# One flag of the tile scheduler: the order of every engine's instructions built with its timeline account of time

## The chip, the cores and the metric

The kernel runs on one core of one Trainium2 chip. The metric is the device time of one execution in microseconds (us). The core has five engines that matter here: TensorE (PE in the profile, with its weight loads as PEld), VectorE (DVE), ScalarE (ACT), GpSimd (POOL) and SyncE (SP), which here only issues DMAs. Each engine works through a list of instructions of its own, and waits on semaphores where it needs another engine's result.

## What is computed

A decoder block of depth 1 over a sequence of 1024 tokens of width 1024, in f32:

```
z = rms_norm(h, ln_mix_g) @ w_in
y_sgu  = sgu_group(z[..., :1536], ...)
y_rwkv = rwkv7_group(z[..., 1536:], ...)
h = h + concat([y_sgu, y_rwkv]) @ w_out
h = h + mem_cross_attention(h, mem, ...)
return rms_norm(h, ln_f_g)
```

The part that sets the order of work is `rwkv7_group`: 8 heads of 64, each with a 64x64 state that is carried from token to token:

```
sa = einsum('bhvk,bhk->bhv', state, a)
state = state * w + sa[..., None] * bb + v[..., None] * k
y = einsum('bhvk,bhk->bhv', state, r)
```

## The kernel before, in words

**Dense products.** Every large matrix product is split in three: both operands are divided into a high and a low part (`split`, L156 on ACT and L157 on DVE), and `mm3` (L177 to L179) issues three matmuls of 128x512 or 128x256 into a PSUM tile `mm`, of which there are three. There are 3216 such matmuls in the program. They are called dense products here. The stages are: keys and values of the memory, input norm and the first projections; the SGU group; the RWKV group with the rest of the input projection and the first part of the output projection (`out_proj`); then the rest of `out_proj` with the folding of the key weights (`k_fold`), the folding of the value weights, and the attention over eight blocks of tokens.

**The RWKV group.** The work is cut into four pairs of heads and two halves of the sequence, eight pieces that follow each other; a piece is called a half here. A half has eight chunks of 64 tokens. `serial` carries the state through the chunks, 64 chunks in all, each in three steps that depend on each other:

```
nc.tensor.matmul(us[:, 0, :], ra[:, c, :, :], s_old, ...)      # L766, then DVE L768 makes ab
nc.tensor.matmul(us[:, 1, :], tt[...], ab, ...)                # L775, then ACT L776 makes avt
nc.tensor.matmul(us[:, 2, :], bkt[:, cq, :], avt[:, cq, :], ...) # L781, then DVE L787 makes s_new
```

From L766 to L775, from L775 to L781, and from L781 to the next chunk's L766 are called hops. They are 183 in all. What a half needs before its chunks is made one or two halves ahead: `elementwise` (L583 to L636), `grams` (L656 to L684), `turn` (L696, L702) and `solve` (four rounds of small products at L717 with DVE between them). In `grams` the masked blocks go to DRAM and come back in another layout (L665, L672); then 28 small DVE instructions that depend on each other (L677, L679) invert 16x16 blocks after L673, and the result goes to DRAM and back again (L680, L684) before `solve` begins with L725. After a half, `outputs` (L799) and `finish` (L809 to L828) write its rows to `y_scr` in DRAM.

**What sets the order.** The function `drive` calls the generators of these pieces in turn, so that dense products, steps of the chain and the small work are recorded mixed with each other. That is the program order; instruction numbers and the numbers in tile names grow with it. When the `TileContext` of `kernel()` (L1198) is left, a scheduler makes one list per engine out of it: among what its account of time says is ready, what was recorded earlier goes first. It also adds the waits. The lists are fixed when the kernel is built, and an engine does not leave its list's order when an instruction has to wait.

## Time and profile before

| what | value |
|---|---|
| median of 3 runs | 954.45 us (954.15 to 956.72) |
| the profiled execution, its own time | 952.35 us |
| its span in the profile | 950.6 us |
| PE busy | 906.8 us |
| DVE busy | 593.5 us |
| ACT busy | 390.5 us |

The span is from the first to the last instruction; the execution's own time holds 1.75 us more. Busy time is the time in which an engine has at least one instruction under way. Matmuls overlap in the array, so a row's duration of one matmul (0.39 us for a dense product) is longer than the time from its start to the next one's.

### The profile page before, as it was taken

What the parts mean: (1) busy time and instruction counts of PE and PEld (TensorE: products, weight loads), DVE (VectorE), ACT (ScalarE), POOL (GpSimd) and SP (SyncE); (2) the same over time, 40 slices, a digit from 0 to 9 for tenths busy, and PEclk for the clock granted to TensorE, in tenths of its full rate; (3) what the DMA queues carried; (4) which work ended last, traced back from release to release, by engine and by line L of the source; (5) the groups of instructions that cost most, each with busy time, mean ns of one, the idle gap of its engine ahead of it and who ended that gap; (6) DMA issues with size and microseconds to landing.
All of it is one profiled execution on the core that took longest, in us unless ns stands there. A gap on an engine that the chain in (4) does not pass through costs nothing.

```text
span 950.6 us, 16113 instructions
## 1 busy us (share of the span) xinstructions
PE 906.8 (95%) x6236; PEld 728.1 (77%) x6236; DVE 593.5 (62%) x1375; ACT 390.5 (41%) x818; POOL 50.5 (5%) x115
## 2 busy tenths in 40 slices
PE   6989999999999999898989999999799999999996
PEld 6978888888777777676767677677698778888885
DVE  5867233334585878686868789867587664444333
ACT  6763222224442525252616272534266553333222
POOL 0001000012000000000000000000000000000000
PEclk9999999999999999999999999999999999999999
DMA  8862011113122112121111084425462400000001
GB/s 314 264 216 89 23 67 67 67 68 111 40 55 44 37 26 60 26 59 26 48 35 49 24 240 113 115 52 151 143 212 70 136 6 2 26 26 26 26 32 45
DMA packets 86092, 76.86 MB, mean 81 GB/s; under 512 B 38272, under 2 KB 58752, under 8 KB 86016
## 3 DMA queue, kind: packets, MB, share of 16 engines
q1 hardware_dynamic: 84864, 73.73, 24.9%
q10 hardware_dynamic: 1152, 2.10, 0.6%
q8 instruction: 49, 0.80, 0.4%
q14 instruction: 27, 0.22, 0.1%
HBM read 62.17 MB, written 13.64 MB: 80 GB/s over the span
## 4 chain that ended last, share of the span: by engine, by line
PE 78%; DVE 13%; issue 3%; DMA 2%; POOL 2%; ACT 1%; POOLq 0%; SPq 0%; DVEq 0%; ACTq 0%
PE mm L177 21%; PE mm L179 20%; PE mm L178 20%; PE cb L717 3%; PE us L766 2%; PE us L775 2%; PE yps L799 2%; PE us L781 1%; POOL grs L153 1%; DVE gr L666 1%; PE co L717 1%; DVE stdiag L787 1%; DMA w_raw<-in_w_sv 1%; DVE cs L592 1%; PE co L432 1%
## 5 line engine op out<-in xcount | busy, mean ns | idle before, releaser
L177 PE MATMUL mm<-xh,w_hi 128*128 128x512 f32 x400 | 167.2, 418 | 0.0
L179 PE MATMUL mm<-xh,w_lo 128*128 128x512 f32 x400 | 159.8, 400 | 0.0
L178 PE MATMUL mm<-xl,w_hi 128*128 128x512 f32 x400 | 159.5, 399 | 0.0
L157 DVE TENSOR_TENSOR w_lo<-w_raw,w_hi 128x512 fp32r<-128x512 f32 x115 | 78.7, 686 | 63.9 <-ACT w_hi L156 61.4
L156 ACT CAST w_hi<-w_raw 128x512 fp32r<-128x512 f32 x115 | 70.8, 617 | 91.4 <-PE mm L178 75.8
L179 PEld LDWEIGHTS mm<-xh,w_lo 128*128 128x128 f32 x400 | 75.8, 190 | 14.8 <-issue 0.2
L177 PEld LDWEIGHTS mm<-xh,w_hi 128*128 128x128 f32 x400 | 76.0, 190 | 12.9 <-issue 1.0
L178 PEld LDWEIGHTS mm<-xl,w_hi 128*128 128x128 f32 x400 | 76.2, 190 | 12.5 <-issue 0.5
L177 PE MATMUL mm<-wo,w_hi 128*128 128x512 f32 x128 | 54.2, 424 | 0.0
L776 ACT COPY avt<-us 64x128 f32<-64x128 f32 x64 | 16.6, 259 | 90.1 <-PE us L775 89.8
L178 PE MATMUL mm<-wo,w_hi 128*128 128x512 f32 x128 | 52.4, 409 | 0.0
L179 PE MATMUL mm<-wo,w_lo 128*128 128x512 f32 x128 | 51.8, 404 | 0.0
L177 PE MATMUL mm<-vp_h,p_hi 128*128 128x512 f32 x128 | 51.3, 401 | 0.0
L179 PE MATMUL mm<-kp_h,w_lo 128*128 128x512 f32 x128 | 50.1, 391 | 0.0
L177 PE MATMUL mm<-kp_h,w_hi 128*128 128x512 f32 x128 | 50.0, 391 | 0.0
L179 PE MATMUL mm<-vp_h,p_lo 128*128 128x512 f32 x128 | 50.0, 390 | 0.0
L178 PE MATMUL mm<-vp_l,p_hi 128*128 128x512 f32 x128 | 49.9, 390 | 0.0
L178 PE MATMUL mm<-kp_l,w_hi 128*128 128x512 f32 x128 | 49.9, 389 | 0.0
L787 DVE SCALAR_TENSOR_TENSOR stdiag<-us,dc,sd 64x64 f32<-64x64 f32 x112 | 31.6, 283 | 21.9 <-PE us L781 19.4
L772 ACT ACTIVATE sd<-stdiag,dc 128x128 f32<-128x128 f32 x56 | 22.4, 399 | 40.7 <-DVE stdiag L787 37.1
L1040 DVE TENSOR_REDUCE mx<-mm 128x2 f32<-128x512 f32 x16 | 11.1, 691 | 41.8 <-PE mm L179 41.8
L499 ACT ACTIVATE t<-mm,vec 128x512 f32<-128x512 f32 x34 | 23.3, 684 | 33.7 <-PE mm L179 32.7
(272 smaller groups left out, 2029.1 us busy)
## 6 DMA issues: line engine op xcount, KB each, us to landing
w_raw<-in_w_blk SPq DMA_DIRECT2D x50, 256.0 KB, 2.5
w_raw<-y_scr SPq DMA_DIRECT2D x32, 256.0 KB, 3.3
w_raw<-in_w_kv SPq DMA_DIRECT2D x17, 256.0 KB, 3.9
xr<-in_xT SPq DMA_DIRECT2D x8, 512.0 KB, 5.7
w_raw<-in_w_out SPq DMA_DIRECT2D x16, 256.0 KB, 2.8
h_all<-in_x SPq DMA_DIRECT2D x16, 256.0 KB, 4.5
pr<-in_w_qT SPq DMA_DIRECT2D x8, 512.0 KB, 4.4
w_raw<-in_w_o SPq DMA_DIRECT2D x16, 256.0 KB, 2.6
```

The lines of the kernel that those rows point to most:

```text
L156: nc.scalar.copy(out=hi, in_=src)
L157: (eng or nc.vector).tensor_tensor(out=lo, in0=src, in1=hi.bitcast(F32), op=ALU.subtract)
L177: nc.tensor.matmul(ps, lh, rh, start=first, stop=False)
L178: nc.tensor.matmul(ps, lh, rl, start=False, stop=False)
L179: nc.tensor.matmul(ps, ll, rh, start=False, stop=last)
L499: nc.scalar.activation(out=t1[:, 1:HT + 1], in_=ps, func=AF.Copy, scale=vc("mu", b))
L717: nc.tensor.matmul(ps[R[hh], c, :], fl(hh, c), fr(hh, c), start=True, stop=True)
L766: nc.tensor.matmul(us[:, 0, :], ra[:, c, :, :], s_old, start=True, stop=True)
L772: nc.scalar.activation(out=sd, in_=s_old, func=AF.Copy, scale=dcc)
L775: nc.tensor.matmul(us[:, 1, :], tt[:, c - c % 2:c - c % 2 + 2, :], ab, start=True, stop=True)
L787: nc.vector.scalar_tensor_tensor(out=s_new[h2, h2], in0=us[h2, 2, h2], scalar=dcc[h2], in1=sd[h2, h2], op0=ALU.mult, op1=ALU.add)
L799: nc.tensor.matmul(yps[R[c % 2], o:o + 64], gr[:, c, hh, :], avt[:, c, R[hh]], start=True, stop=True)
```

## The change

`TileContext` takes a flag that says with which account of time the scheduler builds its order. Nothing else is changed: the same instructions are recorded, in the same program order, with the same tiles and buffers. On every engine the two lists hold the same instructions.

```
-    with tile.TileContext(nc) as tc:
+    with tile.TileContext(nc, schedule_with_timeline_sim=True) as tc:
         tile_hybrid_block(tc, *args)
```

All five lists change: a PE instruction stands 58 places from where it stood on average (of 4893), a DVE instruction 21 (of 1377), an ACT instruction 10 (of 770), one of SP 5 (of 330). Three places follow.

The first is PE in the sixth half, from the second step of its second chunk to the third chunk (`us_5659` and `us_5767` are the PSUM tiles of these chunks; `mm_` are dense products, L823 and L799 belong to `finish` and `outputs`). Before:

```order
L775 MATMUL us_5659<-abdiag1_1927,tt_5441 128x128
L179 MATMUL mm_5584<-xh5_104,w_lo_5438 128x512
L177 MATMUL mm_5584<-xh6_105,w_hi_5437 128x512
L178 MATMUL mm_5584<-xl6_113,w_hi_5437 128x512
L781 MATMUL us_5659<-avt_5218,bkt_5219 128x128
L179 MATMUL mm_5584<-xh6_105,w_lo_5438 128x512
L177 MATMUL mm_5584<-xh7_106,w_hi_5437 128x512
L178 MATMUL mm_5584<-xl7_114,w_hi_5437 128x512
L179 MATMUL mm_5584<-xh7_106,w_lo_5438 128x512
L766 MATMUL us_5767<-stdiag0_1924,ra_4821 128x128
```

Now:

```order
L775 MATMUL us_5659<-abdiag1_1927,tt_5441 128x128
L799 MATMUL yps_5958<-avt_5218,gr_5023 64x64 x4
L781 MATMUL us_5659<-avt_5218,bkt_5219 128x128
L766 MATMUL us_5767<-stdiag0_1924,ra_4821 128x128
L775 MATMUL us_5767<-abdiag0_1926,tt_5441 128x128
L799 MATMUL yps_5958<-avt_5218,gr_5023 64x64 x2
L781 MATMUL us_5767<-avt_5218,bkt_5219 128x128
```

The dense products that stood between the steps have moved ahead, into the halves before. Counted over the list, the dense products inside the eight halves were 72, 91, 96, 96, 96, 100, 106 and 81 up to the last step, and are 64, 168, 24, 146, 190, 0, 0 and 96. Before, each of the 63 stretches from one chunk's L775 to the next chunk's held 3 to 28 of them; now 39 of the 63 hold none, and one of the others holds 63. Ahead of the first step stand 1376 dense products in place of 1280, behind the last one 1152 in place of 1198.

The second place is PE behind the last step of the last chunk (`us_7047`; `mm_7094` and the like are `out_proj`, `mm_7195` is the first product of `k_fold`). Before:

```order
L775 MATMUL us_7047<-abdiag1_1927,tt_6571 128x128
L179 MATMUL mm_7094<-wo_6952,w_lo_7031 128x512
L177 MATMUL mm_7094<-wo_6986,w_hi_7030 128x512
L799 MATMUL yps_7054<-avt_6519,gr_6228 64x64 x2
L178 MATMUL mm_7094<-wo_6986,w_hi_7030 128x512
L179 MATMUL mm_7094<-wo_6986,w_lo_7031 128x512
```

Now:

```order
L775 MATMUL us_7047<-abdiag1_1927,tt_6571 128x128
L799 MATMUL yps_7054<-avt_6519,gr_6228 64x64 x2
L823 MATMUL yps_7098<-cst_75,ytok_6706 128x128 x4
L177 MATMUL mm_7195<-ktt0_7177,p_hi_7191 128x256
```

Before, 46 dense products and twelve small transposes of the attention (L1015) stood between L775 of `us_7047` and `mm_7195`; now only L799 and L823 do.

The third place is DVE, where the eighth half's blocks have been masked (L661 to L666) and L673 waits for them to come back from DRAM. Before:

```order
L664 TENSOR_TENSOR ak1_6231<-co_6233,cst_75 64x256
L666 TENSOR_TENSOR gr_6228<-co_6233,cst_75 128x4x64
L768 TENSOR_TENSOR abdiag1_1927<-us_6254,akv_6045 64x64 x2
L666 TENSOR_TENSOR gr_6228<-co_6232,cst_75 128x4x64
L152 TENSOR_SCALAR rs_t_6321<-gsv_6318 128x8
L157 TENSOR_TENSOR w_lo_6365<-w_raw_6362,w_hi_6364 128x512
L819 TENSOR_TENSOR ytok_5577<-ytok_5577,grs_6320 128x512
L787 SCALAR_TENSOR_TENSOR stdiag0_1924<-us_6254,dc_5326,sd_6258 64x64 x2
L872 SCALAR_TENSOR_TENSOR h_all_5893<-mm_6368,s_r_94,h_all_5893 128x512
L768 TENSOR_TENSOR abdiag0_1926<-us_6372,akv_6045 64x64 x2
L157 TENSOR_TENSOR wo_6407<-w_raw_6408,wo_6407 128x512
L826 TENSOR_TENSOR ysq_6316<-ysq_6316,zr_3582 128x512
```

Now:

```order
L664 TENSOR_TENSOR ak1_6231<-co_6233,cst_75 64x256
L768 TENSOR_TENSOR abdiag0_1926<-us_6031,akv_5442 64x64 x2
L763 COPY abdiag0_1926<-akv_6045 64x64 x2
L787 SCALAR_TENSOR_TENSOR stdiag1_1925<-us_6031,dc_4764,sd_6035 64x64 x2
L673 TENSOR_TENSOR nt1_6198<-ak1_6199,cst2_1922 64x256
L677 TENSOR_TENSOR xtmp_6265<-ak1_6199,nt1_6198 64x14
L679 TENSOR_TENSOR nt1_6198<-nt1_6198,xtmp_6265 64x14
L768 TENSOR_TENSOR abdiag1_1927<-us_6105,akv_5442 64x64 x2
```

Before, L673 comes two rows after these twelve. Now it stands four rows behind the last mask (L664), and the chain's next step (L768 of `us_6105`) stands behind L673.

## Rows read from the trace of the kernel before

**Rows 1.** The page, part 1: busy time and share of each engine.

```profile
PE 906.8 (95%) x6236; PEld 728.1 (77%) x6236; DVE 593.5 (62%) x1375; ACT 390.5 (41%) x818; POOL 50.5 (5%) x115
```

**Rows 2.** Five stretches of the span: length, busy time by engine, clock, DMA share, GB/s.

```profile
0.00:75.00 75.00, 64.51 (x464) 59.53 (x465) 51.79 (x90) 48.87 (x89) 3.63 (x10) 1.00 0.77 260
75.00:300.60 225.60, 224.82 (x1289) 182.58 (x1287) 108.53 (x216) 70.43 (x118) 15.37 (x43) 1.00 0.18 62
300.60:665.10 364.50, 345.56 (x3151) 260.68 (x3152) 288.79 (x813) 158.03 (x375) 18.22 (x45) 0.99 0.25 70
665.10:690.00 24.90, 18.98 (x95) 15.50 (x94) 14.09 (x24) 7.23 (x15) 1.64 (x1) 0.93 0.47 148
690.00:950.60 260.60, 252.93 (x1244) 209.77 (x1242) 130.29 (x236) 105.90 (x225) 11.69 (x16) 0.99 0.16 54
```

**Rows 3.** Timeline of one chunk: start us, duration us, engine, line, tiles [idle before].

```profile
642.17 0.46 PE L766 MATMUL us<-stdiag,ra 128*128 128x128 f32 x2
642.38 0.48 PE L177 MATMUL mm<-wo,w_hi 128*128 128x512 f32 x1
...
642.70 0.39 PE L178 MATMUL mm<-wo,w_hi 128*128 128x512 f32 x1
...
642.93 0.40 PE L179 MATMUL mm<-wo,w_lo 128*128 128x512 f32 x1
643.19 0.49 PE L775 MATMUL us<-abdiag,tt 128*128 128x128 f32 x2
...
644.20 0.47 PE L781 MATMUL us<-avt,bkt 128*128 128x128 f32 x2
...
645.46 0.35 PE L766 MATMUL us<-stdiag,ra 128*128 128x128 f32 x1
```

**Rows 4.** Chain of waits: start us, us, engine, tile, line, matmuls merged.

```profile
282.20 1.08 PE co L717 x32
...
285.03 2.06 PE co L656 x31
...
367.81 0.61 PE yps L799 x14
```

**Rows 5.** Groups of DVE instructions by line: count, busy us, mean ns, idle before.

```profile
L787 DVE SCALAR_TENSOR_TENSOR stdiag<-us,dc,sd 64x64 f32<-64x64 f32 x112 | 31.6, 283 | 21.9 <-PE us L781 19.4
L768 DVE TENSOR_TENSOR abdiag<-us,akv 64x64 f32<-64x64 f32 x120 | 27.2, 226 | 11.0 <-PE us L766 8.9
L679 DVE TENSOR_TENSOR nt<-nt,xtmp 64x14 f32<-64x14 f32 (+6 forms) x112 | 21.2, 189 | 1.4
```

**Rows 6.** Timeline of DVE and SP around the two round trips to DRAM.

```profile
396.22 0.57 SPq L665 DMA_DIRECT2D nt_scr<-an  x1
...
401.64 0.58 DVE L673 TENSOR_TENSOR nt<-ak,cst 64x256 f32<-64x256 f32 x1
...
416.74 0.15 DVE L679 TENSOR_TENSOR nt<-nt,xtmp 64x14 f32<-64x14 f32 x1
...
425.43 0.70 DVE L725 STREAM_TRANSPOSE tt<-t 128x512 f32<-128x512 f32 x1
```

**Rows 7.** Timeline of PE behind the last chunk.

```profile
665.09 0.38 PE L775 MATMUL us<-abdiag,tt 128*128 128x128 f32 x2
...
673.89 0.63 PE L823 MATMUL yps<-cst,ytok 128*128 128x128 f32 x4 [0.80 <-DVE ytok L819]
...
684.25 0.35 PE L177 MATMUL mm<-ktt,p_hi 128*128 128x256 f32 x1 [4.97 <-DMA w_raw<-y_scr]
```

**Rows 8.** Stretches around a fall of the clock, and one step in it.

```profile
394.40:397.80 3.40, 1.10 (x6) 0.70 (x5) 2.50 (x8) 0.21 (x1) 0.00 (x0) 1.00 0.17 36
397.80:401.20 3.40, 3.40 (x11) 2.65 (x11) 1.38 (x4) 1.28 (x4) 0.28 (x2) 0.50 0.22 22
...
543.50:546.90 3.40, 1.69 (x10) 0.96 (x8) 2.64 (x8) 0.52 (x2) 0.00 (x0) 1.00 0.09 19
...
398.32 0.65 PE L781 MATMUL us<-avt,bkt 128*128 128x128 f32 x2
```

## The prediction, made before the result was known

> **What bounds the kernel now.** I began with the page's busy times [rows 1]: PE is at work for 906.8 of 950.6 us, so a reorder can give back at most the 43.8 us in which it is not. Then I cut the span into five stretches to see where those lie [rows 2]. The start loses 10.5 us (75.00 - 64.51) while the loads run at a DMA share of 0.77; the projections lose 0.8; the stretch from the first to the last step of the chain (300.6 to 665.1) loses 364.5 - 345.6 = 18.9; the 25 us behind it lose 5.9; the rest 7.7, most of it after the last matmul. PE is the bound almost everywhere, and the chain is hidden under it.
>
> How much cover the chain needs is seen in one chunk [rows 3]. L766 starts at 642.17, L775 at 643.19, L781 at 644.20, the next L766 at 645.46: hops of 1.02, 1.01 and 1.26 us, 3.29 for a chunk, with next to nothing waiting in between. 364.5 us for 63 chunks is 5.8 each, so before the chain needs only a little over half of its time.
>
> **The stretch of the chain.** I priced every product on PE by its start-to-start time. A dense product takes 0.23 us (642.70 to 642.93), a chain product about 0.33 with the slower dense product behind it [rows 3]; 16 products at L717 take 1.08, so 0.07 each; one at L656 0.13; one at L799 0.085 [rows 4] (there the x counts two passes per product). DVE's instructions I priced at their own durations, the chain's share being 2 x 0.283 + 2 x 0.226 = 1.02 us per chunk [rows 5]. For each chunk, from L766 to L766, I then took the longest of four: PE's work, DVE's work, ACT's work, and 3.29.
>
> With the old lists this rule gives 38 chunks led by PE, 20 by DVE, 2 by ACT, 3 by the chain, and 364.1 us in all, against 364.5 in the trace [rows 2]. PE's work in it is 342.7, so PE lacks work for 21.4. (The 18.9 above count overlap as busy; I use 21.4 on both sides.) With the new lists it gives 24 chunks led by PE (218.6 us), 21 by DVE (130.1 us, with only 76.7 of PE work), 17 by the chain (55.9 us, 29.5 of PE work) and 1 by ACT (4.3, 4.1 of PE work): 408.9 us with 328.8 of PE work, so 80.1 idle. **Term 1: 80.1 - 21.4 = +58.7 us.** It counts idle PE time; the 13.9 us of PE work that left the stretch are done elsewhere and cancel.
>
> Its floor is the hops alone. With the old lists 15 of the 183 hops have less PE work than the hop lasts, short by 1.6 us together; with the new lists 84, short by 48.8 (0.58 each). If nothing else held PE up, the term would be 48.8 - 21.4 = +27.4.
>
> **Behind the last chunk.** From L775 at 665.09 to the first product of `k_fold` at 684.25 the path through `finish`, `y_scr` and the next loads takes 19.2 us, of which PE shows 4.97 + 0.80 idle [rows 7]. The 46 dense products and 12 transposes that covered it are gone ahead, and 1.1 us of PE work is left in it: 18.1 idle, so +12.3. The lower end is zero, if the path shortens by as much. DVE has nothing of another phase left between these steps, so it will be somewhat shorter. **Term 2: +10.**
>
> **The two round trips to DRAM.** From the last store of masked blocks at 396.22 to L673 at 401.64 are 5.4 us; from the end of the inversion (416.74) to L725 are 8.7 [rows 6]. DVE takes its list in order, so whatever stands behind L673 or L725 waits with it, the chain's L768 too. In the new list none to six chain instructions and 1.4 to 2.4 us of DVE work stand ahead of L673, which is at most a bare chunk, 3.29: 2.1 short, in eight halves 17. Ahead of L725 it is about 4.5 short in three halves, 3 in two, and covered in the others: 19.5. The 36 us are the upper end; the lower is 0, where dense products cover them. Since 24 of 63 stretches still hold dense products, I take half. **Term 3: +18.** L680 and the loads behind it also stand in SP's list and share these waits; the PE work that depends on them is ahead by then, so I add nothing.
>
> **The clock.** After 394.4 to 397.8, where PE was busy for 1.10 of 3.40 us, the granted clock was 0.50 (1.2 GHz) for the next 3.4 us; after 1.69 of 3.40 at 543.5 it stayed at 1.00 (2.4 GHz) [rows 8]. A bare chunk holds three chain products and two to four small ones in 3.3 to 5 us, like the first of these. At 0.50 a chain pair lasts 0.65 [rows 8] in place of 0.47 [rows 3]: 3 x 0.18 x 39 chunks = 21 us if all run so, 0 if none. **Term 4: +10.5, half.**
>
> The Trainium skill (TensorE: Matmul & The Clock Gate, What's actually happening) states that the throttled state is the default and that activity releases it. By it all 39 bare chunks would run at 1.2 GHz and the sum would be 10 us higher. The trace speaks for less, since it kept 2.4 GHz after the second stretch.
>
> **Fewer changes between kinds of product.** A dense product behind a small one takes 0.32 us to the next start (642.38 to 642.70) in place of 0.23 [rows 3]. There are 254 such changes in the old list and 114 in the new. Those around the chain are in term 1 already; of the others 115 become 86. **Term 5: 29 x 0.09 = -2.5.**
>
> What I cost at nothing. The start: its loads are issued in a slightly different order, but nothing is added, and the DMA share bounds it from both sides; -3 to +3. The attention at the end: the same products back to back. The dense bursts: up to 63 products, 14 us, in one go, which need ACT and DVE to split weights and empty PSUM. In the stretch of projections the same dense work keeps PE full with ACT busy for 70.4 and DVE for 108.5 of 225.6 us [rows 2]. If that cover failed, each burst would stall for a PSUM tile, some us in all.
>
> **Sum.** 58.7 + 10 + 18 + 10.5 - 2.5 = 94.7, on a span of 950.6: 1045.3. With the 1.75 us around the span it is 1047.1 for the profiled execution, and as the median of the runs shown lies 2.1 above that execution (954.45 against 952.35), **1049 us** for the median.
>
> **The rivals.**
> - *Only the hops cost* (chance 0.13). DVE's work fits beside the bare hops, the round trips come in time, the clock stays up. 954.45 + 27.4 + 10 = 992. For it: the hop in [rows 3] waits for nothing but its own steps. Against it: 20 chunks already follow DVE's work before.
> - *Everything waits* (0.25). All of the round trips and all of the low clock are on the path: 1049 + 18 + 10.5 = 1078. For it: in the sixth and seventh half PE has no dense product to be late with, so every wait there is the kernel's. The Trainium skill's rule (TensorE: Matmul & The Clock Gate, What's actually happening) points this way for the clock's part.
> - *Faster, by fewer changes between kinds* (0.04). In the chain's stretch PE changes from a small product to a dense one 140 times less; at 0.09 us that is 12.6 us, 942. It decides once the 84 short hops cost less than 12.6 together, 0.15 us each. They are 0.58 short each by the trace, and PE takes its list in order, so I see no way to it except that dense products reach PE earlier than I count.
> - *It changes nothing that is on the path* (0.02). The lists differ on every engine, and 39 bare stretches cannot be hidden by an engine that has nothing to run, so this needs gains that cancel the losses: 954.
>
> My own case has 0.56.
>
> **Range and chances.** 0.3%, about 2.9 us, is what a measurement of this kernel can tell from no change. Faster: the third rival, 0.04. Same: 0.02. Slower: the rest, 0.94. The range starts at the floor (992, rounded to 990, so that the first rival is in) and ends a little above the second rival, 1085, which leaves out the rivals at and below 954 and some of the tails.
>
> **What would show it.** In the changed profile PE's busy time falls by a few us only, while the span grows by 60 to 130; the idle time lies between the first L766 and the last, in pieces of about 0.5 to 1 us in front of L775, L781 and L766, and is thickest in the sixth and seventh half. PE's waits on DVE (L768, L787) and on ACT (L776) grow to tens of us. L673 and L725 show idle time on DVE ended by a DMA (term 3). One gap of 10 to 17 us lies ahead of the first product of `k_fold` (term 2). The clock is at 0.50 for several stretches in the chain (term 4). I am wrong if the bare stretches take under 3.3 us a chunk, if PE's idle time in the chain stays under 40 us, or if the time is lost in the dense bursts or at the start.

## The result, and the profile after

The changed kernel takes **1078.59 us** (median of 4 runs, 1075.24 to 1081.12) against 955.45 for the kernel before in the same job: ratio 1.1287, 95% interval 1.1247 to 1.1327, slower by 123 us. The forecast was 1049 in a range of 990 to 1085. Sign and place were right, the size was 30 us short. The profiled execution took 1080.15 us with a span of 1078.4, that is 127.8 more than the span before; the sums below are made on the spans. Medians are of the fast executions: one of eight of `early_l768`, the profiled one, took 2623.84 us, with PE's matmuls more than twice as long, and is left out, so this kernel has no trace to compare.

The page, part 1, of the changed kernel, as [rows 1]:

```profile
PE 981.1 (91%) x6236; PEld 794.2 (74%) x6236; DVE 605.1 (56%) x1375; ACT 394.0 (37%) x818; POOL 49.7 (5%) x115
```

PE is busy for 74.3 us more with the same 6236 matmuls. I had expected its busy time to fall a little and all of the loss to show as idle time. Idle time grows by 53.5 us only (43.8 to 97.3). The rest is in matmuls that last longer or no longer overlap with a neighbour: a busy PE is not the same as a PE that gets more done.

The same five stretches as [rows 2], cut at the first and last L775 of this trace (clock, DMA share and GB/s are the last three columns):

```profile
0.00:75.00 75.00, 65.19 (x462) 59.61 (x463) 50.32 (x85) 48.84 (x88) 2.42 (x9) 1.00 0.78 260
75.00:319.90 244.90, 243.35 (x1407) 199.74 (x1406) 119.03 (x235) 76.95 (x128) 16.52 (x50) 1.00 0.19 61
319.90:789.00 469.10, 409.57 (x3093) 316.06 (x3092) 296.14 (x807) 155.38 (x366) 17.37 (x39) 0.83 0.20 54
789.00:815.00 26.00, 9.77 (x43) 8.24 (x44) 10.66 (x17) 7.79 (x14) 1.64 (x1) 0.54 0.47 149
815.00:1078.00 263.00, 253.24 (x1237) 210.56 (x1235) 129.00 (x233) 105.04 (x222) 11.71 (x16) 0.99 0.16 51
```

The start is unchanged. Ahead of the chain 96 more dense products take their 22 us (96 x 0.23) and no more. The chain's stretch is 469 us in place of 364.5 although 50 dense products have left it, and its mean clock is 0.83 in place of 0.99. PE's busy time in it rises from 345.6 to 409.6 us, its idle time from 18.9 to 59.5. In the 26 us behind the last chunk PE works for 9.77, at a clock of 0.54.

Cut by halves, from L775 to L775 of every eighth chunk, with each dense product taken off at 0.23 us (the counts are those of the lists; the eighth column ends with the last L775; all lengths in us, and the last row is the time at a granted clock of 0.50, which is 1.2 GHz):

| half | 1 | 2 | 3 | 4 | 5 | 6 | 7 | 8 |
|---|---|---|---|---|---|---|---|---|
| length before | 42.9 | 44.0 | 50.3 | 49.8 | 48.4 | 51.5 | 48.6 | 28.8 |
| length after | 58.7 | 74.6 | 48.8 | 68.8 | 83.2 | 42.2 | 41.0 | 51.4 |
| dense before / after | 72 / 64 | 91 / 168 | 96 / 24 | 96 / 146 | 96 / 190 | 100 / 0 | 106 / 0 | 81 / 96 |
| without dense, before | 26.3 | 23.1 | 28.2 | 27.7 | 26.3 | 28.5 | 24.2 | 10.2 |
| without dense, after | 44.0 | 36.0 | 43.3 | 35.2 | 39.5 | 42.2 | 41.0 | 29.3 |
| low clock after | 16.6 | 14.1 | 17.1 | 14.2 | 11.5 | 25.1 | 34.2 | 24.0 |

Every half loses 7.5 to 19 us, 116 in all, those with bursts as well as those with nothing dense. In a half with bursts the dense work stands in a few chunks and leaves the others bare.

PE's waits in the changed kernel: line, what it waited for, us in total, times, longest.

```profile
PE us L775 <- DVE abdiag L768: 20.4, 24, 2.2
PE us L766 <- DVE stdiag L787: 14.7, 20, 1.2
PE mm L177 <- ACT w_hi L156: 10.4, 6, 5.9
PE mm L177 <- DMA w_raw<-y_scr: 9.6, 1, 9.6
PE yps L823 <- DVE ytok L819: 7.2, 4, 6.3
```

And in the kernel before:

```profile
PE us L775 <- DVE abdiag L768: 8.6, 4, 2.3
PE mm L177 <- ACT w_hi L156: 8.2, 3, 6.0
PE mm L177 <- DMA w_raw<-y_scr: 5.0, 1, 5.0
PE us L766 <- DVE stdiag L787: 4.4, 8, 1.0
PE yps L823 <- DVE ytok L819: 2.1, 2, 1.3
```

The waits of the chain's own steps have grown most, 24 and 20 times in place of 4 and 8. The bursts of dense products stall little: the wait for split weights (L156) grows by 2.2 us.

And two of VectorE's waits, in front of L673 and L725, whose round trips were seen in [rows 6]:

```profile
DVE nt L673 <- DMA ak<-nt_scr: 10.6, 6, 3.0
DVE tt L725 <- DMA t<-t_img: 8.5, 5, 4.1
```

The kernel before has one such wait, ahead of the chain:

```profile
DVE tt L725 <- DMA t<-t_img: 5.4, 1, 5.4
```

In the changed kernel 4.4 us of them lie ahead of the chain too (3.0 in front of L673, 1.4 in front of L725); 14.6 lie in the chain.

Two bare chunks in a row show the clock's part. This is PE's timeline at the end of the eighth half; it answers to [rows 3]:

```profile
779.29 0.46 PE L766 MATMUL us<-stdiag,ra 128*128 128x128 f32 x2 [0.52 <-DVE stdiag L787]
780.31 0.49 PE L775 MATMUL us<-abdiag,tt 128*128 128x128 f32 x2 [0.56 <-DVE abdiag L768]
781.15 0.45 PE L799 MATMUL yps<-avt,gr 128*64 128x64 f32 x4 [0.35 <-ACT avt L776]
781.53 0.49 PE L781 MATMUL us<-avt,bkt 128*128 128x128 f32 x2
782.78 0.76 PE L766 MATMUL us<-stdiag,ra 128*128 128x128 f32 x2 [0.77 <-DVE stdiag L787]
784.12 0.80 PE L775 MATMUL us<-abdiag,tt 128*128 128x128 f32 x2 [0.58 <-DVE abdiag L768]
785.26 0.69 PE L799 MATMUL yps<-avt,gr 128*64 128x64 f32 x4 [0.35 <-ACT avt L776]
785.89 0.80 PE L781 MATMUL us<-avt,bkt 128*128 128x128 f32 x2
787.46 0.77 PE L766 MATMUL us<-stdiag,ra 128*128 128x128 f32 x2 [0.78 <-DVE stdiag L787]
```

The granted clock in these stretches:

```profile
779.00:782.10 3.10, 1.81 (x10) 1.20 (x10) 0.65 (x4) 0.92 (x3) 0.00 (x0) 0.99 0.00 0
782.10:785.50 3.40, 1.80 (x6) 1.24 (x7) 0.97 (x4) 0.82 (x3) 0.00 (x0) 0.50 0.00 0
785.50:788.90 3.40, 2.04 (x9) 1.37 (x8) 1.02 (x4) 0.00 (x0) 0.00 (x0) 0.50 0.00 0
```

Both chunks hold the same products. At 2.4 GHz the chunk takes 3.49 us (779.29 to 782.78), which is close to the 3.29 of [rows 3]; at 1.2 GHz it takes 4.68 (782.78 to 787.46). The waits for VectorE and ScalarE are the same in both; the chain products are longer, by 0.30 to 0.31 each, and L799 by 0.24, together 1.16 of the 1.19.

Behind the last chunk, as [rows 7]:

```profile
788.81 0.80 PE L775 MATMUL us<-abdiag,tt 128*128 128x128 f32 x2 [0.58 <-DVE abdiag L768]
...
796.92 1.09 PE L823 MATMUL yps<-cst,ytok 128*128 128x128 f32 x4 [6.27 <-DVE ytok L819]
807.61 0.55 PE L177 MATMUL mm<-ktt,p_hi 128*128 128x256 f32 x1 [9.61 <-DMA w_raw<-y_scr]
```

### The profile page after: what moved, and what is told of

Its sections match the earlier page's. It is cut to its first block, busy times and chain, and to the rows that moved or that the text cites. A ratio compares the mean times of both kernels' runs of the same rounds, so it can differ in the third digit from the quotient of the medians.

```text
span 1078.4 us, 16178 instructions
## 1 busy us (share of the span) xinstructions
PE 981.1 (91%) x6236; PEld 794.2 (74%) x6236; DVE 605.1 (56%) x1375; ACT 394.0 (37%) x818; POOL 49.7 (5%) x115
## 3 DMA queue, kind: packets, MB, share of 16 engines
q10 hardware_dynamic: 1152, 2.10, 0.5%
## 4 chain that ended last, share of the span: by engine, by line
PE 76%; DVE 9%; DMA 7%; ACT 3%; issue 3%; POOL 0%; SPq 0%; POOLq 0%; DVEq 0%; ACTq 0%
PE mm L177 19%; PE mm L179 19%; PE mm L178 19%; PE cb L717 4%; PE co L656 2%; PE yps L799 2%; PE us L781 2%; PE us L775 2%; PE us L766 2%; DMA w_raw<-y_scr 1%; DMA ak<-nt_scr 1%; DMA xr<-in_xT 1%; DVE stdiag L787 1%; DVE abdiag L768 1%; PE yps L823 1%
## 5 line engine op out<-in xcount | busy, mean ns | idle before, releaser
L177 PE MATMUL mm<-xh,w_hi 128*128 128x512 f32 x400 | 161.6, 404 | 1.6 <-DVE zr L503 1.6
L156 ACT CAST w_hi<-w_raw 128x512 fp32r<-128x512 f32 x115 | 71.1, 619 | 112.5 <-PE mm L178 90.7
L177 PEld LDWEIGHTS mm<-xh,w_hi 128*128 128x128 f32 x400 | 76.9, 192 | 18.2 <-DVE zr L503 2.2
L178 PEld LDWEIGHTS mm<-xl,w_hi 128*128 128x128 f32 x400 | 76.8, 192 | 16.6 <-issue 1.2
L775 PE MATMUL us<-abdiag,tt 128*128 128x128 f32 x128 | 36.9, 379 | 20.6 <-DVE abdiag L768 20.4
L178 PE MATMUL mm<-vp_l,p_hi 128*128 128x512 f32 x128 | 49.8, 390 | 0.0
L775 PEld LDWEIGHTS us<-abdiag,tt 128*128 128x128 f32 x128 | 25.5, 240 | 30.0 <-DVE abdiag L768 27.2
L766 PE MATMUL us<-stdiag,ra 128*128 128x128 f32 x120 | 33.4, 369 | 14.9 <-DVE stdiag L787 14.7
```

Of the source, the lines that this page charges most:

```text
L156: nc.scalar.copy(out=hi, in_=src)
L177: nc.tensor.matmul(ps, lh, rh, start=first, stop=False)
L178: nc.tensor.matmul(ps, lh, rl, start=False, stop=False)
L766: nc.tensor.matmul(us[:, 0, :], ra[:, c, :, :], s_old, start=True, stop=True)
L775: nc.tensor.matmul(us[:, 1, :], tt[:, c - c % 2:c - c % 2 + 2, :], ab, start=True, stop=True)
```

## The experiments

Lists can be fixed without the flag: a helper gives each instruction of an engine a dependency, without a semaphore, on the one that a table names as its predecessor. The edit is the same in all kernels of this kind, and only the tables differ:

```
     with tile.TileContext(nc) as tc:
         tile_hybrid_block(tc, *args)
+        _order(nc, tc, TABLES)
```

**Is it the lists, and whose?** First all five new lists under the old scheduler.

> The old scheduler with all five engine lists fixed by tables to the lists of the changed kernel; nothing else of the flag is left. If the lists alone make the time, it is the changed kernel's: 1074 to 1083 us. If the flag does something beside the lists (other places in memory, other waits), it differs from that by more than 5 us. It is also what the next kernels are compared with.

Measured: 1077.48 us, ratio 1.1269 (1.1238 to 1.1301). The lists alone make the time. Of the 63 chunk lengths 53 repeat between the two traces to 0.1 us, so later kernels can be compared chunk by chunk with this one. The other ten differ by up to 1.6 us, most of them where the low clock begins or ends at another place.

Then PE's new list alone, `TABLES = {"PE": new}`.

> The old scheduler, and only PE's list fixed to the new one; VectorE's, ScalarE's, GpSimd's and SyncE's lists are what the old scheduler makes of that. Theory A (the 39 chunks that lose their dense products on PE are the loss, whichever order the other engines have): 1050 to 1090, the low clock comes back too. Rival B (the loss is in the lists of the other engines: DVE taking L673 and L725 too early, transfers issued late): 954 to 985.

Measured: 1129.80 us, ratio 1.182 (1.1788 to 1.1852). More than both theories said. But this kernel is no test of PE's list alone, because the other lists follow it: what is ready on VectorE hangs on what PE has done. Matched instruction by instruction in the traces, VectorE's order here is on average 2.2 places from that of the changed kernel and 20 from the old one, ScalarE's 0.4 and 10. So it doesn't tell A from B. It shows that these small shifts cost 52 us over the lists that belong together: PE waits 16.8 us at L823 in place of 7.2, and 14.1 at L717 for `t_img` in place of 3.0.

Then the reverse: the flag on, `TABLES = {"PE": old}`.

> The flag is on, and only PE's list is fixed to the old one; the other four engines get the order of the timeline account. Theory A (PE's list makes the loss): 945 to 975, PE's idle time in the chain stretch under 30 us, hardly any time at the low clock. Rival B (the other lists make it): over 1030. Between them, 975 to 1030, both hold a part.

Measured: 988.84 us, ratio 1.0334 (1.03 to 1.0368). Between the two. PE's old list, and what follows it on the other engines, takes back 88.6 of the 122 us. The 33 that stay are not the price of the changed kernel's other four lists: VectorE's order here is on average 2.5 places from the old one and 20 from the new. They are the price of the small shifts that the timeline account makes around PE's old list. VectorE's waits in this kernel, whose loads are the subject of the next paragraph:

```profile
DVE tt L725 <- DMA t<-t_img: 16.0, 6, 6.8
DVE nt L673 <- DMA ak<-nt_scr: 10.5, 6, 3.5
```

**The round trips to DRAM.** The loads read what the half before stored, so that the kernel leaves out the wait for the half's own stores: once with all lists as in the run just told (`pe_old_trips`), once with the five new lists (`trips`).

```
             ns, ti = nt_scr[i % 2], t_img[i % 2]
+            ns_old, ti_old = (nt_scr[(i - 1) % 2], t_img[(i - 1) % 2]) if i else (ns, ti)
...
-            nc.sync.dma_start(out=L, in_=diag(ns))
+            nc.sync.dma_start(out=L, in_=diag(ns_old))
...
-                                      in_=ti[j, hh, :, 0:C, :].rearrange("c s t -> s c t"))
+                                      in_=ti_old[j, hh, :, 0:C, :].rearrange("c s t -> s c t"))
```

> All five lists as in the run with the old PE list and the new order on the other four engines, but from the second half on the two loads take what the half before had stored, so that L673 and L725 no longer wait for the stores of their own half; the output is computed from the wrong blocks. VectorE stands still 26.5 us there in that run. Theory K (the 33 us that the other four lists cost are these waits, in front of the chain's L768): 10 to 25 us less than 988.8, 964 to 979. Rival L (they are spread over ScalarE's and VectorE's other places): 983 to 990.

Measured: 976.29 us, ratio 1.0229 (1.0204 to 1.0254), 12.6 less. VectorE still waits there (one line more in the file moves the line numbers by one):

```profile
DVE tt L726 <- DMA t<-t_img: 8.3, 5, 6.8
DVE nt L674 <- DMA ak<-nt_scr: 3.7, 4, 1.9
```

Of 26.5 us of waiting 14.5 are gone, and 12.6 of time: 0.87 us per us. Where the other 20 us go was not tried.

> The new lists, but in every half from the second on the two loads (the blocks that L673 reads, the inverse that L725 reads) take what the half before had stored, so that they no longer wait for the stores of their own half; the output is computed from the wrong blocks. Theory E (the round trips are on the path in the bare halves): DVE's 19 us of idle time in front of L673 and L725 go, and 10 to 19 us of the time, 1058 to 1068; the low clock falls too. Rival F (another wait takes their place at once, the next product or DVE's own list): under 5 us, 1072 to 1080.

Measured: 1071.63 us, ratio 1.1224 (1.1192 to 1.1255), 5.9 less than the lists with their trips, at the edge of what the two intervals tell apart. VectorE's waits in `all_new`, and then in this kernel:

```profile
DVE nt L673 <- DMA ak<-nt_scr: 8.9, 7, 3.0
DVE tt L725 <- DMA t<-t_img: 7.0, 5, 3.0
```

```profile
DVE nt L674 <- DMA ak<-nt_scr: 4.5, 2, 2.9
DVE tt L726 <- DMA t<-t_img: 3.0, 3, 1.4
```

They are 8.4 us less, so 0.70 us per us. The loads themselves still come late; only the wait for the stores was taken out. Between E and F, nearer F.

**The low clock.** Products are added in chunks 38 to 57, where the changed kernel has nothing dense, to see what the same chunks take at the full clock. First behind each chain product (the edit written out for its one place, ahead of the first dense product of the eighth half):

```
+            ps = psA.tile([P, 512], F32, name="mm")
+            for _ in range(116):
+                nc.tensor.matmul(ps, whi[0][:, 0:P], lstk[0][:, 0:512], start=True, stop=True)
```

PE's table then places them two by two behind L766, L775 and L781.

> The new lists, with two more products of 128x128 by 128x512 behind each chain product of the sixth and seventh half (chunks 38 to 57, 58 places, 116 products, some 26 us of PE work at the full clock); their results are not used. They keep PE busy where the changed kernel has nothing and runs at the granted clock of 0.50 for 85 of 110 us. Theory C (the low clock lengthens the bare chunks: a lone chain pair 0.78 us there against 0.49 at the full clock, so 0.3 for each of 58): the low clock goes from these two halves, they get 10 to 20 us shorter in spite of the added work, 1058 to 1070. Rival D (the bare chunks are bound by DVE, by the order of the steps and by the trips to DRAM, and the clock costs next to nothing there): no gain, and up to 26 us more, 1078 to 1105.

Measured: 1079.11 us, ratio 1.1278 (1.123 to 1.1327). By its time rival D. But the 20 chunks mix two things: several of the light ones got shorter in spite of the added work (chunk 49 from 4.49 to 3.69 us, 50 from 5.03 to 4.23, 57 from 4.93 to 4.27), and the ones with much work of their own longer (44 from 6.25 to 7.65, 51 from 6.17 to 8.29). So the products were moved in front of L766 and L775, where PE stands still.

> The new lists, with added products of 128x128 by 128x512 (results unused) in chunks 38 to 57, this time in front of the chain products, where PE stands still for DVE: three in front of each L766, two in front of each L775, 97 in all, some 22 us at the full clock. Theory C (a bare chunk at the granted clock of 0.50 is 0.3 to 0.9 us longer than the same chunk at the full clock): the bare chunks with next to no other work on PE (39 to 42, 49, 50, 54 to 57) get shorter by 0.3 to 1.0 each although PE has more to do in them; the chunks with much small work of their own (43 to 45, 51 to 53) get longer by 0.5 to 1.5; together 97 to 105 us for the 20 chunks in place of 104.5, and 1065 to 1078 in all. Rival D (the clock is worth nothing, DVE and the order set every chunk): no chunk gets shorter, 105 to 115 for the 20.

Measured: 1076.17 us, ratio 1.1273 (1.1237 to 1.1308); 105.0 us for the 20 chunks. The light chunks get shorter as C said (41 from 4.87 to 4.17, 49 to 3.98, 50 to 3.75, 57 to 3.79), some with much work of their own longer (44 from 6.25 to 7.40). Not all went as C said: 39, 42 (7.79 to 9.89) and 56, which it had among the light ones, got longer, and 52, among the heavy ones, shorter (7.24 to 5.56). The third version leaves the heavy ones alone.

> The new lists with the added products in front of L766 (three) and L775 (two) again, but only in those of the chunks 38 to 57 that have next to nothing else on PE (not in 42 to 45, 51 and 52): 67 products, some 15 us at the full clock, all in places where PE stood still. Theory C (the granted clock of 0.50 costs a bare chunk 0.3 to 0.9 us): the 20 chunks take 96 to 101 us in place of 104.5, and the time falls by 3 to 9 us, 1068 to 1074. Rival D: 104 to 110 and no gain, 1076 to 1084.

Measured: 1074.33 us, ratio 1.1243 (1.1219 to 1.1268), 3.2 less than without the products; the intervals overlap. The trace is clearer. Chunks 38 to 57 in `all_new` and in this kernel, with PE's and VectorE's busy time and the clock:

```profile
638.90:743.40 104.50, 80.19 (x643) 60.25 (x643) 63.82 (x202) 31.60 (x86) 5.18 (x4) 0.63 0.08 19
```

```profile
641.00:741.20 100.20, 81.64 (x709) 59.46 (x709) 63.74 (x202) 31.70 (x86) 5.17 (x4) 0.90 0.09 20
```

66 recorded matmuls more, VectorE's work unchanged, the clock at 0.90 in place of 0.63, and the 20 chunks 4.3 us shorter. Chunk 40 falls from 5.36 to 4.34, 41 to 4.16, 49 to 3.98, 50 to 3.76, 57 to 3.80, and the dense stretch behind them (58) from 11.02 to 9.63, with no low clock in it in place of 8.0 us (the next one, 59, is longer, 16.30 to 17.05). Chunk 51, which got no added product, falls from 6.17 to 5.71 as its low clock goes. Others are longer: 38 (4.24, now 5.15), 39 (7.55, now 8.21), 53 (3.94, now 4.46) and 56 (4.45, now 4.80). Neighbours share such gains and losses, so groups tell more: 48 to 50 take 12.6 us in place of 14.9 and 54 to 57 16.3 in place of 18.2, which is nearly all of the gain; 38 to 41, where VectorE is busy for 16.9 us, take 21.9 in place of 22.0. D falls: PE has more to do in the 20 chunks, and they are shorter. C's price holds for some of the bare chunks and not for those that VectorE leads.

**One bare half in the old order.** The tables hold the new order up to the first L775 and the old one from there (`new_to_0`): 96 dense products go ahead, 72 of the first half and 24 of the second, and some small work with them. The rest of the chain keeps the old order on every engine.

> All five lists are the new ones up to the first chain product at L775 and the old ones from there: 1376 dense products ahead of the chain in place of 1280, so that the first nine or ten chunks have none, and everything else in the chain as before. Theory A (a bare chunk costs 1.5 to 2 us over what its dense products were worth, whichever order the other engines have): 12 to 20 us slower than before, 967 to 976. Rival G (bare chunks are cheap, some 3.3 us, as long as DVE and ACT keep the old order; the loss is in the new order of the small work): 950 to 958.

Measured: 977.04 us, ratio 1.0232 (1.0211 to 1.0253), 21.8 slower, a little more than A said. G falls. The first half in this kernel, and then in the kernel before:

```profile
320.10:367.60 47.50, 37.59 (x327) 27.96 (x325) 29.24 (x94) 14.49 (x38) 0.21 (x2) 0.64 0.08 13
```

```profile
300.70:343.60 42.90, 41.77 (x420) 30.80 (x420) 36.03 (x106) 19.56 (x47) 0.81 (x6) 1.00 0.16 40
```

Without its 72 dense products (16.6 us) the half should take 26.3 us if nothing were lost; it takes 47.5, with PE idle for 9.9 and the clock at 0.64, though VectorE has 6.8 us less to do. That is 21.2 us. The second half begins with two chunks that have lost 24 of their 26 dense products:

```profile
367.64:412.25 44.61, 38.96 (x396) 30.22 (x394) 33.05 (x98) 18.82 (x45) 2.40 (x7) 0.92 0.18 44
```

It takes 44.6 us with 67 dense products in place of 44.0 with 91, so it loses 6.1. The span grows by 23.4; some 4 of the 27.3 come back elsewhere, most of them ahead of the chain. So the old order of the small work doesn't save bare chunks.

**The eighth half and the drain.** New order up to chunk 56, old from there.

> All five lists are the new ones up to the first L775 of the eighth half (chunk 56) and the old ones from there: the dense products of the last half stand again one group per hop, and 46 of them behind the last chunk. Theory A with term 2 (bursts of up to 63 in some chunks, none in others and none behind the last one): of the 51.4 us of the last half and the 289.0 behind it 18 to 30 come back, 1047 to 1060. Rival H (the drain behind the last chunk costs the same with or without cover, the eighth half is no slower than its products): under 10 us, 1067 to 1078.

Measured: 1065.03 us, ratio 1.1148 (1.1126 to 1.117), 12.5 less, between A and H. In the trace the eighth half goes from 51.4 to 32.3 us and what is behind it from 289.0 to 285.6, 22.5 together, as A said. The cut itself costs 7.2 us in the seventh half (41.1 to 48.3), where the left-over small work is bunched: chunk 55 holds 42 PE instructions in place of 10 and takes 12.56 us in place of 5.04. The 24 us behind the last chunk are again like those of [rows 2, 7]:

```profile
777.80:802.00 24.20, 18.16 (x89) 14.66 (x88) 14.04 (x24) 7.37 (x14) 1.64 (x1) 0.93 0.48 146
```

**A version that beats both.** In the old lists PE stands still four times, 1.7 to 2.3 us each, for an L768 that is behind L819 and the masked blocks in VectorE's list. One of the four moves:

```
+L768 TENSOR_TENSOR abdiag_1927<-us,akv 64x64 x2
 L819 TENSOR_TENSOR ytok<-ytok,grs 128x512
 L663 TENSOR_TENSOR nt_3920<-co,cst 64x256
...
 L661 TENSOR_TENSOR an<-co,cst 128x256
 L666 TENSOR_TENSOR gr<-co,cst 128x4x64
-L768 TENSOR_TENSOR abdiag_1927<-us,akv 64x64 x2
```

> The lists of the kernel before, with one change on VectorE: in the third to sixth half the L768 that stands behind L819 and the masked blocks (L663, L664, L666, L661) is taken ahead of L819. Before, PE stands still for it four times, 2.30, 2.31, 2.31 and 1.71 us, while VectorE waits 1.75 us for GpSimd in front of L819 with L766 long done. Theory I (in a bound PE every such wait is the kernel's): 5 to 10 us faster, 945 to 950. Rival J (the products behind it then wait for the masked blocks or for PSUM instead): 952 to 957.

Measured: 950.76 us, ratio 0.995 (0.9932 to 0.9968): faster by half a per cent, clear of 1 by its interval: 4.9 us of the 8.6. Then with two more kinds of step:

```
-L813 ACTIVATE ysq<-ytok 128x512
-L776 COPY avt<-us 64x128
+L776 COPY avt<-us 64x128
+L813 ACTIVATE ysq<-ytok 128x512
```

> As the kernel with L768 taken ahead of L819, and two more kinds of chain step moved ahead in the old lists: on VectorE L787 ahead of L503 in five halves (PE stood still 0.63 to 0.67 us for it in four of them and 0.37 in the fifth), on ScalarE L776 ahead of L813 in the fourth to sixth half (0.61 and 0.75 us in two of them). Of PE's 8.6 us in front of L775 the first edit gave back 4.8 in time; these places hold 4.3 us more. Theory I: 2 to 4 us below the kernel with the first edit alone (950.8), 946.5 to 949, and PE shows no wait over 1 us for L768 between 350 and 600. Rival J (the small work that is pushed back becomes the next wait): 949.5 to 953, with new waits of PE for the masked blocks or for PSUM.

Measured: 949.13 us, ratio 0.9939 (0.9924 to 0.9953), at the border of I and J. PE's waits in this kernel:

```profile
PE us L766 <- DVE stdiag L787: 6.1, 8, 1.4
...
PE us L775 <- DVE abdiag L768: 2.4, 5, 0.9
...
PE co L656 <- DVE gr L666: 1.8, 3, 0.7
```

The wait for L768 is down from 8.6 us to 2.4. Part of it comes back one step later: L766 now waits 6.1 us in place of 4.4, up to 1.4 at a time, and L656 up to 0.7 for the masked blocks that were pushed back. The profiled execution was the longest of the six (952.91 us). In it the chain's stretch takes 360.7 us in place of 364.4, and the stretch ahead of the chain, which the edits don't touch, 303.5 in place of 300.7.

## Why the prediction was right, and where it fell short

The case was the right one: bare chunks in the chain, a drain without cover, late round trips, a lower clock. `new_to_0` shows the bare chunks and their lower clock alone, with one bare half and the start of the next, and the old order on every engine from there.

**Term 1 (+58.7), right within the rule's own error.** The rule "the longest of PE's, VectorE's and ScalarE's work and 3.29 us" can be held against each of the 62 stretches from the second L775 on. Where the clock was full the 29 stretches take 249.1 us, and the rule gives 240.3. Where it was low for part or all of a stretch the 33 stretches take 205.4, and the rule gives 159.8. So where the clock was full the rule is 9 us short in 249, and the low stretches hold the rest. It is not better than that: counted in this way, from L775 to L775, it gives 378.4 for the kernel before, where the trace has 359.1. That it came to 364.1 against 364.5 in the prediction was partly luck with where the chunks were cut. The rival that only the hops cost falls with this.

**Term 2 (+10), right, slightly low.** Behind the last L775 PE is idle for 26.4 us up to the end in place of 13.5, so +12.9; the upper end was 12.3. From the last L775 to the first product of `k_fold` it takes 18.8 us (788.81 to 807.61) in place of 19.2, so the path hardly shortens. `new_to_56` gives the cover back, and the idle time is 13.4 again. The low clock lasts to 812.8, which makes the first products of `k_fold` slower too: net of the 46 products that left (10.6 us), the stretch behind the chain is 14.7 us longer.

**Term 3 (+18), right in kind, too high.** VectorE shows 19.1 us of such waits, 14.6 of them in the chain, where the kernel before has none. At 0.70 to 0.87 us of time per us of wait, as the two experiments gave, the 14.6 are an estimate of 10 to 13.

**Term 4 (+10.5), the step that failed.** The low clock lasts 189.1 us in the changed kernel, 156.8 of them in the chain, against 15.5 before, 6.8 of them in the chain. The direction was right, but both factors were too small. The price was 3 x 0.18 per chunk, from a pair that had a dense product behind it [rows 3, 8]. Alone, a pair takes 0.76 to 0.80 at 1.2 GHz and 0.46 to 0.49 at 2.4, and L799 pays too, so the neighbours above differ by 1.19: 0.25 us for each us at the low clock. For 156.8 us that is an estimate of 40. And I took only bare chunks, and half of them. In the trace 19 of the 39 have the low clock throughout or nearly so, 8 in part and 12 hardly or not at all, and 36 us of low clock lie in stretches with dense products, behind a bare group. `fillc` shows the effect on the same chunks, but not its whole size: in chunks 38 to 58 it took 65 us of low clock away, and 5.7 us of time with 67 added products in the way.

The 40 is an estimate from one chunk that holds little beside the chain, and the price differs from chunk to chunk. The traces of the changed kernel and of `all_new` have the same lists, but the low clock falls at other places in them. Chunk 18, with 24 dense products, and chunk 24, a bare one, in the first and then in the second:

```profile
464.80:475.85 11.05, 11.05 (x60) 8.88 (x61) 7.42 (x15) 3.42 (x8) 0.30 (x2) 0.70 0.14 47
502.25:506.44 4.19, 2.36 (x6) 1.50 (x6) 3.63 (x15) 2.28 (x7) 1.64 (x1) 0.50 0.01 2
```

```profile
464.68:474.18 9.50, 9.50 (x60) 7.78 (x61) 7.25 (x15) 3.43 (x8) 0.30 (x2) 0.82 0.09 30
500.10:504.19 4.09, 1.75 (x7) 1.10 (x7) 3.63 (x15) 2.27 (x7) 1.64 (x1) 0.75 0.01 2
```

Chunk 18 has 3.3 us less at the low clock and is 1.55 shorter, 0.47 for each; chunk 24 has 2.2 less and is 0.1 shorter, 0.05 for each (VectorE is busy for 3.63 of its 4.19 us). Other bare chunks that can be compared so lie between nothing and 0.36. At 0.47 for the 36 us in stretches with dense products, and at 0.05 to 0.25 for the 121 in bare ones, the estimate is 23 to 47. All of that lies above my upper end of 21.

What tempted me was [rows 8], where PE was busy for 1.69 of 3.40 us and the clock stayed at 1.00. In the eighth half above it is busy for 1.81 of 3.10, and the next 3.4 us run at 0.50. One stretch that kept the clock was no ground for taking half. The Trainium skill's rule (TensorE: Matmul & The Clock Gate, What's actually happening), that activity releases the throttle, I had read as putting all 39 at 1.2 GHz. That reading was nearer in size than my half, though 12 of the 39 stayed at the full clock.

**Term 5 (-2.5), not shown.** Ahead of the chain 320.1 us in place of 300.7, less 22.1 for 96 dense products, is -2.6. (The term's own product, 29 x 0.09, is 2.6 too.) That is of the term's size, but the same stretch with the same lists takes 319.5 to 321.3 us from trace to trace (`fillb`, `all_new`) and 303.5 with the old lists in `early_chain`, so nothing here shows it.

Together: the chain's 468.7 us are 59.8 above the rule's 408.9, 54.4 of it in the 62 stretches above and the rest in the first. By the estimates above the round trips explain some 10 to 13 of them and the clock some 40 (23 to 47); I had put 28.5 there. What remains is within the rule's own error, and the shares are estimates: no kernel took the low clock, or all the round trips, out of the whole chain. The time came out at that of the rival that everything waits, 1078, but by chance and not by its shares: it had 36 for the trips and 21 for the clock.

One thing was not in the prediction at all: shifts of two or three places on average in the lists beside PE's cost 33 us around PE's old list (`pe_old`) and 52 around its new one (`pe_new`). The terms held for the set of five.

## What to carry to other kernels

A chain that is hidden under dense work needs that work in every hop: dense products that are moved ahead of it are not lost, but each chunk without them costs the hop's wait and then, at 1.2 GHz, up to a third more on top (4.68 in place of 3.49 us). When a reorder makes PE sparse, price the sparse stretches and what follows them at the lower clock, with durations of lone products at that clock. And in lists that are already good, look for a step of the chain that stands behind a long wait of another phase in an in-order queue; moving four such steps was worth 0.5%. And fixing one engine's list does not isolate it: the scheduler makes the others to fit, so look how far they have moved before you put a loss down to one list.

## What the runs showed that I had not expected

- A chunk of the same content took 3.49 us at a granted clock of 0.99 and 4.68 right behind it at 0.50, with the same waits for VectorE and ScalarE.
- The clock fell behind 3.1 us in which PE was busy for 1.81, and stayed up behind 3.4 us with 1.69 [rows 8].
- Two kernels with the same lists repeat most single chunks to 0.1 us (49: 4.49 and 4.49, 50: 5.03 and 5.03, 57: 4.93 and 4.93) while their times spread over 3 to 6 us. Chunk by chunk a trace tells differences that medians don't, except where the low clock falls at another place.
- The price of the low clock depends on what a chunk holds: 0.47 us for each us at 0.50 in a stretch with 24 dense products, 0.05 in a bare one, 0.25 in one with little beside the chain.
